# A hybrid encoder layer: the output projection in seven block products, with weight sums formed by GpSimd during attention

## The chip, the cores and the metric

The kernel runs on one core of one Trainium2 chip. The time is device microseconds of one execution; the time of a kernel is the median of its runs. The engines are TensorE (PE, with its weight loads as PEld), VectorE (DVE), ScalarE (ACT), GpSimd (POOL) and SyncE (SP); the last two and ScalarE can issue DMA transfers, which 16 DMA engines carry out.

## The reference

A layer of a streaming encoder on 512 tokens of width 2048, with 16 learned meta tokens ahead of them. The normed input is multiplied by an input matrix; its columns feed two mixers side by side. The first is a Mamba-2 state-space mixer with 32 heads (convolution over time, decay, chunks of 64 tokens), the second a windowed attention with 16 query heads, 4 key heads and sinks. Their outputs, 2048 and 1024 wide, are set side by side and multiplied by the output matrix:

```
mix = concat([y, att])            # 512 tokens x 3072
out = mix @ w_out                 # 3072 x 2048
h = h + rmsnorm(out, norm_post_w) # norm over the 2048 columns of a token
```

All data are float32 and the products must keep nearly that precision.

## The kernel before

**Precision.** Every large product is made of three matmuls on TensorE: each operand is split into hi (rounded to the type float32r) and lo (the rest), and hi x hi, hi x lo and lo x hi are accumulated in one PSUM bank. Weights come in chunks of 128x1024 (512 KB). `load` (L114) issues a chunk's DMA on SP's queue into one of two `st` buffers, `split_w` (L126) lets ScalarE cast it to `hi` (L132) and VectorE subtract `lo` (L133), each with three buffers. `use(n)` (L137) hands out chunk n, splits up to chunk n+2 and loads up to n+4.

**Stages.** A prologue norms and transposes the input. Then 68 tiles of 128 columns of the input projection follow, two chunks each (`project`, L166, matmuls at L157): 4 for keys and values, 16 for queries and gates of the 8 pairs of attention heads (the attention stage), then 48 for the state-space mixer (the SSD stage: per group a tile for cT, one for bT and two each for x and z). Small matmuls of attention and SSD run between these tiles as tasks: a generator gives up control with the planned time until its next piece, `tick` (L101) moves a planned clock on with every group of projection matmuls, and `wake` runs the tasks that are due. This fixes the order in which instructions are handed to the scheduler of the kernel's language, which allots buffers and places each instruction on its engine's in-order queue, where an instruction that could start early may be placed ahead of others. The `steps` task (L386) works out decays on VectorE and ScalarE at the start of attention. In the SSD stage `conv` (L615) copies a tile from PSUM to one of two buffers `ub`, forms four taps on VectorE into a buffer with the tag cT, bT or xs, and uses the buffer `th` for a tanh (L627), which VectorE multiplies in (L628). These buffers lie in the pool `vpool`, which the attention stage uses only at its start (dtT in an xs buffer). GpSimd issues the loads of rows R (L674) and ev (L717) and does one multiplication per SSD unit, `xe` (L713).

**Output projection.** The mixers' outputs lie in 24 tiles `mix[k]` of 128 features x 512 tokens, attention first. For each of four blocks of 512 columns (r), for each of 12 weight chunks (two rows of 128 features) and four tiles of 128 tokens, three matmuls of 128x512 accumulate into four banks (L880); `splitting` (L779) makes hi and lo of `mix` once. At the end of a block VectorE multiplies by the weights of the norm and ScalarE squares and sums (L894, L895); with the last block the inverse root follows, and a scaling with the residual added and the output's store (`finish`, L839; L850, L851).

Of the kernel before, what the change touches and what calls it, by code (L numbers as in the profile page):

```python
# [7 lines left out]
F32 = mybir.dt.float32  # L8
# [19 lines left out]
NST = 2  # L28

# [14 lines left out]
def hybrid_layer(ctx, tc, x, pre, npre, w_in, w_dt, par, w_out, npost, cst, out):  # L44
# [65 lines left out]
    NCH = NCI + 4 * (NKO // 2)  # L110
    staged, ready = {}, {}
    nload, nsplit = [0], [0]

    def load(upto):  # L114
        while nload[0] < min(upto, NCH):
            n = nload[0]
            st = wpool.tile([P, 1024], F32, tag="st", bufs=NST, name=f"st{n}")
# [19 lines left out]
    def use(n):  # L137
        split_w(n + (2 if n == NCI else 3))
        load(n + 3 + NST)
# [361 lines left out]

    keys(0, pieces0)
# [9 lines left out]
    def attend(hp, pieces):  # L512
# [82 lines left out]
        m = mapool.tile([P, S], F32, tag="m", bufs=8, name=f"ma{hp}")  # L595
        nc.vector.scalar_tensor_tensor(m, av, 0.5, gates[hp], ALU.mult, ALU.mult)
        mix[hp] = m
# [12 lines left out]
    ub = [vpool.tile([P, T + 3], F32, name=f"ub{i}") for i in range(2)]  # L610
# [22 lines left out]
    pools = {}  # L633
# [54 lines left out]
    def unit_task(u_, xs, cT):  # L688
# [84 lines left out]
        nc.vector.reciprocal(sq, sq)  # L773
        for v, yt in ((u_ - 1, y0), (u_, yy)):
            m = pools["y"].tile([P, S], F32, tag="m", bufs=16, name=f"my{v}")
            nc.vector.scalar_tensor_tensor(m, yt, hw[:, v:v + 1], sq, ALU.mult, ALU.mult)
            mix[8 + v] = m

    def splitting(ks):  # L779
        for k in ks:  # L780
            mh[k] = o_pool(k).tile([P, S], F32R, name=f"mh{k}")
            ml[k] = o_pool(k).tile([P, S], F32R, name=f"ml{k}")
            nc.scalar.copy(mh[k], mix[k])  # L783
            nc.vector.tensor_tensor(ml[k], mix[k], mh[k].bitcast(F32), ALU.subtract)
# [31 lines left out]
    mh, ml = [None] * NKO, [None] * NKO  # L816
    vpool.release()
    xpool.release()
    o1 = ctx.enter_context(sb("o1", reuse_waits="tile"))
    o2 = []  # L820
    xr = [None] * NT

    def o_pool(k):
        if k < 16:
            return o1
        if not o2:
            assert not tasks
            pools["s"].release()
            o2.append(tc.alloc_tile_pool(name="o2", bufs=1, side="right", reuse_waits="tile"))
        return o2[0]  # L830

    with tc.high_priority(offset=400):
        splitting([0, 1])
    npw = ssq = None
    ot = {}
    n3 = None
    NC = NKO // 2

    def finish(t, jk):  # L839

        b = 3
        rs = o1.tile([P, 2], F32, tag="ors", bufs=4, name=f"ors{t}")
        nc.vector.tensor_reduce(rs[:, 0:1], ssq[:, t, 0:3], AX.X, ALU.add)
        nc.vector.tensor_scalar(rs[:, 0:1], rs[:, 0:1], 1.0 / D, EPS, ALU.mult, ALU.add)
        nc.scalar.activation(jk, pss[t], AF.Square, accum_out=ssq[:, t, 3:4])
        nc.scalar.activation(rs[:, 1:2], ssq[:, t, 3:4], AF.Sqrt, bias=rs[:, 0:1], scale=1.0 / D)
        nc.vector.tensor_tensor(ot[b, t], pss[t], npw[:, b * 512:(b + 1) * 512], ALU.mult)
        nc.vector.reciprocal(rs[:, 1:2], rs[:, 1:2])
        for b in range(4):
            nc.vector.scalar_tensor_tensor(ot[b, t], ot[b, t], rs[:, 1:2], xr[t][b], ALU.mult, ALU.add)  # L850
            nc.sync.dma_start(out[t * P:(t + 1) * P, b * 512:(b + 1) * 512], ot[b, t])  # L851

    for r in range(4):
        b = r
        toks = range(NT)
        pool = wk if b % 2 else pj
# [120 lines left out]
```

## Time and profile before

| | |
|---|---|
| median of 3 runs | 1204.9 us (1203.27 to 1205.04) |
| the profiled execution | 1202.08 us |
| its span, first to last instruction | 1200.3 us |
| mean granted clock of TensorE | 0.998 |
| busy: PE, DVE, ACT, POOL | 99%, 56%, 37%, 4% |
| moved by DMA | 125.53 MB, of them 12.59 MB on GpSimd's queue |

The profile is of one execution. Its own time is a little over its span, as work before the first and after the last instruction is counted. A busy share is a mean over stages. The granted clock is given as a share of the full clock, 2.4 GHz.

### The profile page before, as it was taken

The numbers are of one execution on the slowest core, as the hardware profiler recorded it, in microseconds if no ns is written. First come the engines' busy times: TensorE is split into PE (matmuls) and PEld (weight loads), VectorE is DVE, ScalarE is ACT, GpSimd is POOL, SyncE is SP. The second block draws the span as 40 slices with busy tenths as digits, with TensorE's granted clock in tenths as the row PEclk, the third lists the DMA queues.
The fourth block names the chain that finished last, engine by engine and source line by source line (L and its number), as shares of the span: only waits on it lengthen the run. The fifth ranks groups of instructions, "written<-read, shape, count | busy, mean of one in ns | idle before, by whom it ended". The sixth has DMA issues, their size and how long they took to land.

```text
span 1200.3 us, 18242 instructions
## 1 busy us (share of the span) xinstructions
PE 1188.5 (99%) x7565; PEld 1057.5 (88%) x7565; DVE 676.5 (56%) x1196; ACT 442.9 (37%) x754; POOL 48.6 (4%) x84
## 2 busy tenths in 40 slices
PE   9999999999999999999999999999999999999997
PEld 7998888888999989999999899998997888888886
DVE  7655555555556766757658566676666923232325
ACT  7544544445322423324234233242332612121212
POOL 0000000000000001010000000100100000000000
PEclk9999999999999999999999999999999999999999
DMA  6222222222333233233332332323332432323534
GB/s 240 94 93 88 72 87 71 71 88 85 111 104 115 83 103 107 87 115 97 106 100 95 106 106 88 118 92 105 100 98 79 150 94 99 97 97 99 165 102 178
DMA packets 37044, 125.53 MB, mean 105 GB/s; under 512 B 4705, under 2 KB 5345, under 8 KB 36705
## 3 DMA queue, kind: packets, MB, share of 16 engines
q1 hardware_dynamic: 32864, 111.78, 28.4%
q0 software_dynamic: 4096, 12.59, 3.5%
q8 instruction: 59, 0.97, 0.3%
q14 instruction: 23, 0.19, 0.0%
q10 hardware_dynamic: 2, 0.01, 0.0%
HBM read 120.03 MB, written 4.33 MB: 104 GB/s over the span
## 4 chain that ended last, share of the span: by engine, by line
PE 95%; DVE 2%; ACT 1%; DMA 1%; issue 0%; DVEq 0%; SPq 0%; ACTq 0%
PE pa L157 46%; PE po L880 22%; PE pb L157 16%; PE yd L722 1%; PE av L590 1%; PE stp L732 1%; PE yo L745 1%; PE ptp L572 1%; PE xt L228 1%; PE sc L542 1%; PE cbp L649 1%; PE xp L702 1%; PE sc L541 1%; PE stp L730 1%; PE nw L295 0%
## 5 line engine op out<-in xcount | busy, mean ns | idle before, releaser
L133 DVE TENSOR_TENSOR lo<-st,hi 128x1024 fp32r<-128x1024 f32 x182 | 222.7, 1224 | 378.3 <-ACT hi L132 371.5
L157 PE MATMUL pa<-xh,hi 128*128 128x272 f32 (+2 forms) x1088 | 373.4, 343 | 0.0
L132 ACT CAST hi<-st 128x1024 fp32r<-128x1024 f32 x182 | 191.4, 1052 | 471.0 <-PE po L880 169.3
L157 PE MATMUL pa<-xl,hi 128*128 128x272 f32 (+2 forms) x1088 | 365.0, 335 | 0.0
L157 PE MATMUL pa<-xh,lo 128*128 128x272 f32 (+2 forms) x1088 | 364.6, 335 | 0.0
L157 PEld LDWEIGHTS pa<-xh,hi 128*128 128x128 f32 x1088 | 205.7, 189 | 23.5 <-issue 3.9
L157 PEld LDWEIGHTS pa<-xh,lo 128*128 128x128 f32 x1088 | 205.5, 189 | 20.4
L157 PEld LDWEIGHTS pa<-xl,hi 128*128 128x128 f32 x1088 | 205.7, 189 | 18.1
L157 PE MATMUL pb<-xh,lo 128*128 128x256 f32 x576 | 162.8, 283 | 0.0
L157 PE MATMUL pb<-xh,hi 128*128 128x256 f32 x576 | 162.7, 283 | 0.0
L157 PE MATMUL pb<-xl,hi 128*128 128x256 f32 x576 | 162.7, 282 | 0.0
L880 PE MATMUL po<-hi,mh 128*128 128x512 f32 x384 | 149.5, 389 | 1.2 <-ACT mh L783 1.2
L880 PE MATMUL po<-lo,mh 128*128 128x512 f32 x384 | 149.4, 389 | 0.0
L880 PE MATMUL po<-hi,ml 128*128 128x512 f32 x384 | 148.9, 389 | 0.0
L157 PEld LDWEIGHTS pb<-xh,hi 128*128 128x128 f32 x576 | 108.5, 188 | 1.0
L157 PEld LDWEIGHTS pb<-xl,hi 128*128 128x128 f32 x576 | 108.4, 188 | 0.0
L157 PEld LDWEIGHTS pb<-xh,lo 128*128 128x128 f32 x576 | 108.4, 188 | 0.0
L880 PEld LDWEIGHTS po<-hi,mh 128*128 128x128 f32 x384 | 72.1, 188 | 16.3 <-ACT mh L783 1.4
L880 PEld LDWEIGHTS po<-hi,ml 128*128 128x128 f32 x384 | 72.1, 188 | 15.1
L880 PEld LDWEIGHTS po<-lo,mh 128*128 128x128 f32 x384 | 72.1, 188 | 14.9
L626 DVE SCALAR_TENSOR_TENSOR cv<-ub,pr,cv 128x528 f32<-128x528 f32 (+1 forms) x96 | 73.4, 764 | 2.4
L627 ACT ACTIVATE ct<-cv 128x528 f32<-128x528 f32 (+1 forms) x32 | 20.5, 641 | 67.0 <-DVE cv L626 66.9
(210 smaller groups left out, 1067.8 us busy)
## 6 DMA issues: line engine op xcount, KB each, us to landing
st<-in_w_in SPq DMA_DIRECT2D x136, 512.0 KB, 3.7
st<-in_w_out SPq DMA_DIRECT2D x48, 512.0 KB, 3.6
R<-scr POOLq DMA_DIRECT2D x32, 256.0 KB, 3.7
x<-in_x SPq DMA_DIRECT2D x8, 512.0 KB, 8.5
ev<-scr POOLq DMA_DIRECT2D x32, 128.0 KB, 3.0
out<-o SPq DMA_DIRECT2D x16, 256.0 KB, 2.4
xr<-in_x SPq DMA_DIRECT2D x8, 256.0 KB, 6.0
npw<-in_npost SPq DMA_DIRECT2D x1, 1024.0 KB, 4.2
```

Source lines behind the costliest of these rows:

```text
L132: nc.scalar.copy(hi, st)
L133: nc.vector.tensor_tensor(lo, st, hi.bitcast(F32), ALU.subtract)
L157: nc.tensor.matmul(ps, wt, xt[k][:, a:b], start=(k == 0 and j == 0), stop=(k == NKT - 1 and j == 2))
L228: nc.tensor.transpose(tp[:, kk, :], xts[j][:, k * P:(k + 1) * P], ident)
L541: nc.tensor.matmul(sv[:, c, o0:o1], lq, kh[:, kv, t0:t0 + o1 - o0], start=True, stop=False)
L542: nc.tensor.matmul(sv[:, c, o0:o1], lq, kl[:, kv, t0:t0 + o1 - o0], start=False, stop=True)
L572: nc.tensor.transpose(tp[:, sl * P:(sl + 1) * P], src, ident)
L590: nc.tensor.matmul(av[h * 64:h * 64 + 64, j * P:(j + 1) * P], lt, rh, start=(s_ == 0), stop=(s_ == 1))
L626: nc.vector.scalar_tensor_tensor(d, uu[:, tap + c0:tap + T], cw[:, ct, tap:tap + 1], d, ALU.mult, ALU.add)
L627: nc.scalar.activation(th[:, 0:n], d, AF.Tanh)
L649: nc.tensor.matmul(cbp[:, j * P:(j + 1) * P], bT[:, cs], cT[:, cs], start=True, stop=True)
L880: nc.tensor.matmul(pss[t], a[k][:, cs], w_, start=(k == 0 and i == 0), stop=(k == NKO - 1 and i == 2))
```

## The change

The product of the 512 x 3072 `mix` and the 3072 x 2048 weights is cut into two halves along each of its three dimensions: tokens (LO and HI, 256 each), features (12 tiles each) and columns (1024 each). Instead of the eight products of blocks, seven products of sums of blocks are formed (a Strassen-Winograd scheme), each of 256 tokens x 1536 features x 1024 columns, accumulated in four banks.

- **Weight sums.** Four of the seven products need sums of weight blocks. The task `weight_sums` is started at the beginning of attention, before `keys(0)`. In 24 steps it loads pieces of the four blocks (128x512, 256 KB each) on GpSimd's queue, adds them there in four operations, and stores each sum to DRAM (`wsum`) from the same queue. It borrows the buffers cT, xs, th or bT, and `ub`, in two alternating sets; the loads of a step are handed out one step ahead. The two `ub` buffers are now made at that point.
- **Weights.** The output projection loads 7 x 12 chunks from `w_out` or `wsum`. Two more `st` buffers come from the pool `o1` once it is open.
- **Activations.** `mix` tiles are now pairs (128 x 2 x 512). `held` forms the sums of activations for each product on VectorE (s1, s2 and in-place differences) and splits the result into `ah` and `al`, up to two pairs of features ahead.
- **Blocks.** `done` combines each finished bank into the blocks of the output: copies on ScalarE after the first product, additions and subtractions on VectorE after the others, then `weigh` (square on ScalarE, weights of the norm on VectorE). Blocks of the first 256 tokens are complete after the sixth product, those of the others after the seventh, and `finish` scales, adds the residual and stores them.

The core of the diff:

```diff
+KH = NKO // 2
-    NCH = NCI + 4 * (NKO // 2)
+    NCH = NCI + 7 * KH
+    wsum = dpool.tile([4, 2, KH // 2, P, 1024], F32, name="wsum")
+    def w_block(rows, cols):
+        return w_out[2 * cols:2 * cols + 2, rows * KH // 2:(rows + 1) * KH // 2]
+    W_SRC = [w_block(0, 0), wsum[1], w_block(1, 0), wsum[0], wsum[2], w_block(1, 1), wsum[3]]
     def load(upto):
...
+            if n % 4 > 1 and "o" in pools:
+                st = pools["o"].tile([P, 1024], F32, tag="st", bufs=2, name=f"st{n}")
+            else:
+                st = wpool.tile([P, 1024], F32, tag="st", bufs=NST, name=f"st{n}")
...
-                src = w_out[(n - NCI) // (NKO // 2), (n - NCI) % (NKO // 2)]
+                m = (n - NCI) % KH
+                src = W_SRC[(n - NCI) // KH][m % 2, m // 2]
...
-        load(n + 3 + NST)
+        load(n + 3 + (4 if "o" in pools else NST))
...
+    ub = [vpool.tile([P, T + 3], F32, name=f"ub{i}") for i in range(2)]
+    def weight_sums():
+        w11, w12, w21, w22 = [w_block(r, q) for r in range(2) for q in range(2)]
+        sets = {}
+        def at(n):
+            return n // 2 % 2, n // 4, slice(None), slice(512 * (n % 2), 512 * (n % 2) + 512)
+        def fetch(n):
+            tags = (("cT", 2), ("xs", 2), ("th", 1) if n % 2 else ("bT", 1))
+            v = [vpool.tile([P, T], F32, tag=tag, bufs=bufs, name=f"ws{n}_{m}") for m, (tag, bufs) in enumerate(tags)]
+            sets[n] = [t[:, 0:512] for t in v + [ub[n % 2]]]
+            for to, fr in zip(sets[n], (w22, w12, w11, w21)):
+                if n < 2:
+                    tc.keep_in_program_order(nc.vector.memset(to[:, 0:1], 0.0))
+                nc.gpsimd.dma_start(to, fr[at(n)])
+        fetch(0)
+        yield 5.0
+        for n in range(2 * KH):
+            if n + 1 < 2 * KH:
+                fetch(n + 1)
+            td, tb_, ta, tc_ = sets.pop(n)
+            for m, to, other in ((2, td, tb_), (0, tb_, ta), (1, ta, td), (3, tc_, ta)):
+                nc.gpsimd.tensor_tensor(to, to, other, ALU.add)
+                nc.gpsimd.dma_start(wsum[m][at(n)], to)
+            yield 9.8
+    spawn(weight_sums(), 6.0)
     keys(0, pieces0)
...
+    def sums(i):
+        h1, h2 = mix[i], mix[NP + i]
...
+        nc.vector.tensor_tensor(s1[i], h2[:, :, HI], h1[:, :, HI], ALU.subtract)
+        nc.vector.tensor_tensor(s2[i], s1[i], h1[:, :, LO], ALU.add)
+    def held(p, i):
+        h1, h2 = mix[i], mix[NP + i]
+        if p == 1:
+            sums(i)
+        elif p == 4:
+            nc.vector.tensor_tensor(h1[:, :, HI], h1[:, :, LO], h1[:, :, HI], ALU.subtract)
+        elif p == 5:
+            nc.vector.tensor_tensor(s2[i], s2[i], h2[:, :, LO], ALU.subtract)
+        src = (h1[:, :, LO], s2[i], h2[:, :, LO], s1[i], h1[:, :, HI], s2[i], h2[:, :, HI])[p]
...
+        nc.scalar.copy(ah, src)
+        nc.vector.tensor_tensor(al, src, ah.bitcast(F32), ALU.subtract)
+        return ah, al
+    def weigh(t, b, src):
...
+        nc.scalar.activation(jk, src, AF.Square, accum_out=ssq[:, t, n:n + 1])
+        nc.vector.tensor_tensor(oo[t, b], src, npw[:, b * 512:(b + 1) * 512], ALU.mult)
+    def finish(t, last):
+        nc.scalar.activation(rs[t][:, 1:2], ssq[:, t, 3:4], AF.Sqrt, bias=rs[t][:, 0:1], scale=1.0 / D)
+        nc.vector.reciprocal(rs[t][:, 1:2], rs[t][:, 1:2])
+        for b in [b for b in range(4) if b != last] + [last]:
+            nc.vector.scalar_tensor_tensor(oo[t, b], oo[t, b], rs[t][:, 1:2], xr[t, b], ALU.mult, ALU.add)
+            nc.sync.dma_start(out[t * P:(t + 1) * P, b * 512:(b + 1) * 512], oo[t, b])
+    def done(p, t, b, ps):
+        if p == 0:
...
+            nc.scalar.copy(oo[t, b], ps)
+        elif p == 1:
...
+            nc.vector.tensor_tensor(uu[t, b], ps, oo[t, b], ALU.subtract)
+        elif p == 2:
+            c = oo[t, b]
+            nc.vector.tensor_tensor(c, ps, c, ALU.add)
+            weigh(t, b, c)
+        elif p == 3:
...
+            nc.vector.tensor_tensor(vv[t, b], uu[t, b], ps, ALU.subtract)
+        elif p == 4:
...
+            nc.vector.tensor_tensor(c, vv[t, b], ps, ALU.subtract)
+            nc.vector.tensor_tensor(uu[t, b], ps, uu[t, b], ALU.subtract)
+            weigh(t + 2, b + 2, c)
+        elif p == 5:
...
+            nc.vector.tensor_tensor(c, c, ps, ALU.subtract)
+            weigh(t, b + 2, c)
+            if b == 1:
+                finish(t, 3)
+        else:
...
+            nc.vector.tensor_tensor(c, ps, c, ALU.add)
+            weigh(t + 2, b, c)
+            if b == 1:
+                finish(t + 2, 1)
+    tb = [(t, b) for t in range(2) for b in range(2)]
+    for p in range(7):
+        pss = {v: bank((pj, wk)[p % 2], f"po{p}_{v[0]}{v[1]}") for v in tb}
+        last = 3 if p == 6 else 1
+        order = [(i, t) for i in range(KH - last) for t in range(2)]
+        order += [(i, t) for t in range(2) for i in range(KH - last, KH)]
+        wts = {}
+        for i, t in order:
+            if i not in wts:
+                wts[i] = use(NCI + p * KH + i)
+                if i % 2 == 0:
+                    n = p * NP + i // 2
+                    for m in range(n + 1, min(n + 3, 7 * NP)):
+                        if m not in ops:
+                            ops[m] = held(m // NP, m % NP)
...
+            for kk in range(2):
+                ws = slice(kk * 512, (kk + 1) * 512)
+                for j, (a, w_) in enumerate(((ah, hi), (ah, lo), (al, hi))):
+                    nc.tensor.matmul(pss[t, b], a[:, kk, cs], w_[:, ws], start=(i < 2 and kk == 0 and j == 0),
+                                     stop=(i >= KH - 2 and kk == 1 and j == 2))
...
+            if i >= KH - 2:
+                done(p, t, b, pss[t, b])
```

Here b is `i % 2`: chunk i holds two rows of 128 features (kk) of one block of 512 columns.

## Rows read from the trace of the kernel before

**Rows 1.** The page, part 1: TensorE's busy us, share, instructions.
```profile
PE 1188.5 (99%) x7565; PEld 1057.5 (88%) x7565; DVE 676.5 (56%) x1196; ACT 442.9 (37%) x754; POOL 48.6 (4%) x84
```

**Rows 2.** Busy time by stage: us and instructions by engine, clock, DMA.
```profile
0.00:20.00 20.00, 17.19 (x71) 11.48 (x72) 12.82 (x37) 12.97 (x27) 0.20 (x4) 1.00 0.85 312
55.00:310.00 255.00, 254.91 (x1548) 218.25 (x1547) 139.85 (x308) 125.94 (x286) 4.38 (x8) 1.00 0.27 87
...
930.00:1180.00 250.00, 249.19 (x1099) 206.36 (x1100) 86.88 (x99) 71.04 (x98) 0.00 (x0) 1.00 0.35 112
```

**Rows 3.** Chain that ended last, in time: start us, us, what.
```profile
943.12 249.57 PE po L880 x1101
```

**Rows 4.** Timeline of the end, TensorE and VectorE: start us, us.
```profile
1192.29 0.39 PE L880 MATMUL po<-hi,ml 128*128 128x512 f32 x1
...
1194.23 2.74 DVE L850 SCALAR_TENSOR_TENSOR o<-o,ors,xr 128x512 f32<-128x512 f32 x4
```

**Rows 5.** Groups by line: busy us, mean ns | idle before, releaser.
```profile
L133 DVE TENSOR_TENSOR lo<-st,hi 128x1024 fp32r<-128x1024 f32 x182 | 222.7, 1224 | 378.3 <-ACT hi L132 371.5 <-DMA xr<-in_x 3.6 <-PE ptp L572 2.7
...
L132 ACT CAST hi<-st 128x1024 fp32r<-128x1024 f32 x182 | 191.4, 1052 | 471.0 <-PE po L880 169.3 <-PE pb L157 168.9 <-PE pa L157 65.0
...
L850 DVE SCALAR_TENSOR_TENSOR o<-o,ors,xr 128x512 f32<-128x512 f32 x16 | 11.0, 748 | 0.1
...
L784 DVE TENSOR_TENSOR ml<-my,mh 128x512 fp32r<-128x512 f32 x16 | 10.0, 680 | 0.0
...
L895 DVE TENSOR_TENSOR o<-po,npw 128x512 f32<-128x512 f32 x12 | 8.3, 690 | 5.0 <-ACT ojk L894 5.0
```

**Rows 6.** DMA issues: queue, count, KB, median us to landing.
```profile
R<-scr POOLq DMA_DIRECT2D x32, 256.0 KB, 3.7
...
out<-o SPq DMA_DIRECT2D x16, 256.0 KB, 2.4
```

**Rows 7.** The line that loads weights: min/median/max, issue and landing.
```profile
L122 SPq DMA_DIRECT2D st<-in_w_out x48: 327/327/328, 901.9 to 1167.9; - x48
...
DMA to landing us min/median/max: 3.3/3.6/9.0
```

**Rows 8.** Views of single tiles and lines: ns min/median/max.
```profile
L674 POOL DMA_DIRECT2D R<-scr x32: 538/545/710, 289.5 to 854.1; - x32
...
L713 POOL TENSOR_TENSOR xe<-xd,dte x16: 828/830/1222, 351.9 to 914.4; 128x384 f32<-128x384 f32 x16
...
L626 DVE SCALAR_TENSOR_TENSOR cv<-ub,pr,cv x96: 741/754/1226, 315.8 to 904.5; 128x528 f32<-128x528 f32 x72, 128x512 f32<-128x512 f32 x24
```

**Rows 9.** Groups of VectorE in attention, 200 to 255.26 us.
```profile
L133 DVE TENSOR_TENSOR lo<-st,hi 128x1024 fp32r<-128x1024 f32 x8 | 9.8, 1223 | 16.0 <-ACT hi L132 16.0
...
L557 DVE TENSOR_SCALAR pbuf<-pbuf,sm 128x192 f32<-128x192 f32 (+2 forms) x16 | 3.7, 303 | 0.1
L522 DVE TENSOR_TENSOR qs<-qr,qs 64x512 fp32r<-64x512 f32 x4 | 2.7, 686 | 0.1
...
L471 DVE TENSOR_TENSOR qr<-qr,swq 128x512 f32<-128x512 f32 x2 | 1.4, 694 | 0.1
```

**Rows 10.** Timeline of GpSimd, its first loads and xe.
```profile
299.53 2.07 POOL L717 DMA_DIRECT2D ev<-scr  x4
351.88 0.83 POOL L713 TENSOR_TENSOR xe<-xd,dte 128x384 f32<-128x384 f32 x1 [50.28 <-DVE xd L710]
```

**Rows 11.** Timeline of VectorE in the steps task.
```profile
61.58 0.32 DVE L415 SCALAR_TENSOR_TENSOR da<-dt,ea 128x160 f32<-128x160 f32 x1
```

**Rows 12.** Timeline of VectorE at the first convolution.
```profile
318.84 0.69 DVE L628 SCALAR_TENSOR_TENSOR cv<-ct,cv 128x512 f32<-128x512 f32 x1 [0.50 <-ACT ct L627]
...
321.81 1.22 DVE L133 TENSOR_TENSOR lo<-st,hi 128x1024 fp32r<-128x1024 f32 x1
```

**Rows 13.** Timeline of ScalarE's weight casts, same stretch.
```profile
320.70 1.04 ACT L132 CAST hi<-st 128x1024 fp32r<-128x1024 f32 x1
...
332.25 1.04 ACT L132 CAST hi<-st 128x1024 fp32r<-128x1024 f32 x1
```

More of the change, by code (lines that the diff above doesn't have):

```diff
@@ L607, in hybrid_layer @@
         gates[hp] = gs
-    ub = [vpool.tile([P, T + 3], F32, name=f"ub{i}") for i in range(2)]
     for t in ub:
@@ L632, in hybrid_layer @@
     cdv = cdec.rearrange("p (j h) -> p j h", h=NH)
-    pools = {}
     def open_pools():
@@ L773, in unit_task @@
         nc.vector.reciprocal(sq, sq)
+        mix[4 + g] = pools["y"].tile([P, 2, S], F32, tag="m", bufs=8, name=f"my{g}")
         for v, yt in ((u_ - 1, y0), (u_, yy)):
[L775 to L784, printed above, removed]
+            nc.vector.scalar_tensor_tensor(mix[4 + g][:, v % 2], yt, hw[:, v:v + 1], sq, ALU.mult, ALU.mult)
     for g in range(8):
@@ L834, in hybrid_layer @@
[L834 to L851, printed above, removed]
@@ new lines, in hybrid_layer, with o_tile @@
+    ops = {}
+    with tc.high_priority(offset=400):
+        ops[0] = held(0, 0)
+    npw = o1.tile([P, D], F32, name="npw")
+    nc.sync.dma_start(npw, npost.partition_broadcast(P))
+    ssq = o1.tile([P, NT, 4], F32, name="ssq")
+    uu, vv, oo, xr, rs = {}, {}, {}, {}, {}
+    def o_tile(name):
+        return pools["c"].tile([P, S], F32, name=name)
+    def weigh(t, b, src):
+        n = b if t < 2 else (0, 3, 1, 2)[b]
+        jk = o1.tile([P, S], F32, tag="jk", bufs=1, name=f"jk{t}_{b}")
+        nc.scalar.activation(jk, src, AF.Square, accum_out=ssq[:, t, n:n + 1])
+        nc.vector.tensor_tensor(oo[t, b], src, npw[:, b * 512:(b + 1) * 512], ALU.mult)
@@ new lines, in residual @@
+    def residual(t):
+        pool, nb = (mapool, 4) if t < 2 else (pools["y"], 8)
+        for h in range(2):
+            xq = pool.tile([P, 2, S], F32, tag="m", bufs=nb, name=f"xr{t}_{h}")
+            nc.sync.dma_start(xq.rearrange("p a b -> p (a b)"), x[t * P:(t + 1) * P, h * 1024:(h + 1) * 1024])
+            xr[t, 2 * h], xr[t, 2 * h + 1] = xq[:, 0], xq[:, 1]
+    def finish(t, last):
[4 more added lines that the diff above has]
+            nc.sync.dma_start(out[t * P:(t + 1) * P, b * 512:(b + 1) * 512], oo[t, b])
@@ new lines, in hybrid_layer @@
+    tb = [(t, b) for t in range(2) for b in range(2)]
[13 more added lines that the diff above has]
+                            ops[m] = held(m // NP, m % NP)
+                if p == 5 and i in (0, 2):
+                    residual(i // 2)
+                if p == 6 and i in (2, 4):
+                    residual(1 + i // 2)
+            hi, lo = wts[i]
+            ah, al = ops[p * NP + i // 2]
+            b = i % 2
+            cs = slice(t * P, (t + 1) * P)
+            for kk in range(2):
[3 more added lines that the diff above has]
+                                     stop=(i >= KH - 2 and kk == 1 and j == 2))
+                tick(0.68)
+            if i >= KH - 2:
+                done(p, t, b, pss[t, b])
@@ L907, in hybrid_layer @@
+    pools["c"].release()
     pools["y"].release()
```

99 lines of the change are left out of this document (30 added, 69 removed).

## The prediction

> **What bounds the kernel now.** I read the page first, then busy time by stage, then the chain that ended last, and after that the groups of each engine. TensorE is busy 99% of the span, and the granted clock is 1.00 in each stage read, the 2.4 GHz level [rows 1, 2]. The chain is TensorE almost throughout, and its last long piece is the output projection: 1101 matmuls in 249.57 us without a break, 0.2267 us each; behind the last matmul, which ends at 1192.68, come 7.6 us of VectorE and output stores up to the span's end at 1200.3 [rows 3, 4]. So in this stage time is the number of matmuls, as long as what feeds TensorE keeps up. VectorE is busy there 86.88 of 250 us, GpSimd not at all; in the attention stage GpSimd is busy 4.38 of 255 us and the DMA engines 27% [rows 2]. The change takes work from the one full engine and gives it to idle ones.
>
> **The sum: matmuls.** Before, the projection has 4 x 24 x 4 x 3 = 1152 matmuls, after it 7 products x 12 weight chunks x 2 token tiles x 2 rows of 128 x 3 terms = 1008, all of the same 128x128 by 128x512 shape. 144 x 0.2267 = 32.6 us less, 228.5 us for the stage.
>
> **VectorE in the projection.** Each chunk now feeds 12 matmuls (2.72 us) instead of 24 (5.44 us), and there are 84. VectorE pays 84 lo at 1.22 = 103 us; 42 splits of activations at 0.68 = 29; 24 sums of activations at 0.68 (two for each of six pairs in the second product, one in the fifth and the sixth) = 16; 44 operations on output blocks at 0.69 = 30; 16 last scalings at 0.75 = 12 [rows 5]. That is 190 of 228.5 us, 83% instead of 35%. On the mean it fits; what costs is bunching at the end of a product. Three hi/lo buffers mean that a chunk is split while the chunk two before it runs: two chunks, 5.4 us, less hi 1.05 and lo 1.22, so a lo may come 3.1 us late. From the end of a product's first bank (three banks of 6 matmuls, 4.1 us, before its end) to the need for the third chunk of the next lie 4.1 + 5.4 = 9.5 us. After the sixth product VectorE has there 8 x 0.69 + 8 x 0.75 + 2 x 1.22 + 0.68 = 14.6 us, 5 too many; after the fifth 12 x 0.69 + 2 x 1.22 + 2 x 0.68 = 12.1, 2.6 too many; after the third 8.6. Lost: between 0 (a lo goes ahead of the block work) and 8; I take 3, since recorded durations overlap a little when operations stand back to back (the last four scalings take 2.74 us together, four means 2.99 [rows 4, 5]). ScalarE pays 84 hi at 1.05 and some 0.6 us pieces and is no limit. SP issues 36 loads more at 0.33 us, each [rows 7], about 28 us in all on a queue that issues nothing else but outputs and x there; 512 KB every 2.72 us are 193 GB/s, and at the start of the kernel the DMA engines moved 312 at a share of 0.85 [rows 2].
>
> **The end.** The last bank now needs one addition (0.69) ahead of the square; the multiplication by the weights then runs beside the square instead of behind it (0.3 back): +0.4 us.
>
> **The sums in attention: cost of a step.** There are 24 steps of 4 loads, 4 additions of 128x512 and 4 stores, all on GpSimd's in-order queue, which before holds only the R and ev loads and xe. An addition: xe, 128x384 with two SBUF inputs, is 0.83 us [rows 8], in proportion 1.11 (from 0.83, if all were fixed, to 1.11). An issue of 256 KB from this queue is 0.545 [rows 8]; the rows have only loads on it, and I take a store as the same. 4 x 1.11 + 8 x 0.545 = 8.8 us, a step's floor. Semaphore hops between an addition and its store and back: 8 at 0 to 0.2, no row shows one, I take 0.1: +0.8. Then VectorE. Once xe took 1.222 instead of 0.83 and a cv beside it 1.226 instead of 0.754 [rows 8]: two operations with two SBUF inputs delayed each other. In two rounds of attention, 55.26 us, lo, the pbuf scalings, the second half of qs and the last sum of the rotation, all with SBUF inputs alone, hold VectorE 9.8 + 3.7 + 2.7 + 1.4 = 17.6 us, 32% [rows 9]; an addition that meets one waits up to 1.22 us, about half an operation on the mean: 0.32 x 0.6 = 0.2, +0.8 a step (0 to 4.9). Step: 10.4 us.
>
> The Trainium skill ("SBUF — State Buffer", on the two physically separate sides) says that a VectorE instruction with two SBUF inputs and a GpSimd instruction that reads SBUF exclude each other for the whole instruction. The one late xe agrees in kind: both were stretched by 0.4 to 0.5 us. By that rule at its worst, an addition blocked every time, the step would be 14.5 us instead of 10.4, and the change would lose, as the third rival shows.
>
> **The wait for the buffers.** Two sets of four buffers alternate, so the loads of step n+1 wait for the stores of step n-1 to land. A store of 256 KB from SP lands in 2.4 us, a 256 KB load on GpSimd's queue in 3.7 [rows 6]. If all four loads stand at the head of the step, the fourth waits 0.545 + 3.7 - 3 x 0.545 = 2.6 us at most with all additions behind it. But GpSimd's order isn't that of the code: the ev loads of units 0 and 1 were issued at 299.53, ahead of xe of unit 0 at 351.88 [rows 10]. The planner puts an instruction where it thinks its inputs ready, so an addition should fill the gap: I take 0 and keep 2.6. The stage moves 50.3 MB more in about 260 us, 193 GB/s, beside 87: at 322 GB/s a full share (87 / 0.27) that is 87%. The start of the kernel ran at 85%, and loads there landed in up to 9.0 us instead of 3.6 [rows 2, 7]; the next loads have almost a step, 10 us, so this is hidden.
>
> **Where the chain of sums ends, and what waits for it.** The first loads wait for VectorE's memsets, kept behind the steps task, whose last operation of the first part ran at 61.58 [rows 11]. 61.9 + 3.7 + 24 x 10.4 + 3.7 for the last landing = 319. The borrowed buffers (cT, xs, th, bT, ub) are those of the convolutions. The first one's tanh writes th, and VectorE's operation that waits for it, at 318.84, stands in order ahead of the lo at 321.81 [rows 12]. A chunk's cast runs when the chunk two before it starts, so this chunk, cast at 320.70, is wanted about when the cast two later runs, at 332.25 [rows 13]; its lo ends at 323.03. So 9.2 us of lateness are free: the chain may end at 318.84 + 9.2 = 328, and each microsecond beyond is TensorE's. The first convolution's copies to ub and the R loads behind the sums on GpSimd's queue lie inside the same bound. At 10.4 us a step nothing is lost; the limit is 10.4 + 9 / 24 = 10.8, a narrow margin. What VectorE loses to GpSimd in attention (32% of its time can be blocked by additions that hold 43%) lengthens softmax by 1 to 2 us in a round of 27.6; the hi and lo casts have room. I take 1 us for the stage (0 to 3).
>
> **Sum.** -32.6 + 3 + 0.4 + 1 = -28.2 us on the profiled execution's 1202.1. The median of the runs is 1204.9, 2.8 above it: 1177. No row says that the new kernel would keep that distance; it is within the spread of the runs.
>
> **Rivals.** First, the sums end late by less than the gain: with hops or lock at twice what I took, 11.3 us a step, the end is 61.9 + 3.7 + 271 + 3.7 = 340, 12 past 328: 1189. For it: most terms of a step are estimates and each tenth counts 24 times. Second, VectorE bounds the projection: bunching at each product's end at the upper bound of 8, and as much at its start, where 9 us of the last SSD unit's work are left to it: +10 to 13 on my 3: 1188. Against it: 17% of free time over the stage. Third, on the other side: the wait of the fourth load comes each step, 10.4 + 2.6 = 13.0 us, the chain ends at 381, 53 us late: 1230. It decides where the step exceeds 10.8 + 28 / 24 = 12.0 us. For it: in-order queue, stores and loads slower at 87% DMA share; against it: the planner's freedom shown in [rows 10]. The full lock (14.5 us a step, end 417, 89 us late: 1266) is its far end and hardly likely, since the median xe was not delayed [rows 8]. Fourth, that the change does not do what it says (TensorE's matmuls slower when fed twice as fast, at 0.234 us: 1008 x 0.0073 = 7 us): 1184; nothing in the rows speaks for it.
>
> **Chances and range.** Forecast 0.50; first rival 0.16; second 0.09; third 0.21; fourth 0.04. The forecast's own range is 1171 (nothing bunches, no delay) to 1187 (all bounds short of the late chain). For 8 in 10 I go from 1171 to 1218, which leaves out the far part of the third rival and a little below. Faster by over 0.2% (2.4 us, about what runs of this kernel can tell from no change): the forecast, the first, second and fourth rivals, less the part of the first that comes near 12 us: 0.75. Within: 0.04, slower 0.21.
>
> **What the changed profile would show.** 1008 matmuls of the projection at 0.227; VectorE above 80% there, with TensorE's gaps only behind the fifth and sixth products, waiting for lo. On GpSimd 96 additions of 1.1 to 1.4 us and 192 issues of 0.55, the last between 300 and 328, and no wait of VectorE, ScalarE or TensorE for it behind 310. The prediction is wrong if steps stand 12 us or more apart, if the loads of a step wait for DMA, if TensorE stands still between 320 and 400, or if lo comes late in every product.

## The result and the profile after

The changed kernel takes 1280.8 us (median of 4 runs, 1277.3 to 1283.0), the kernel before 1204.7 in the same comparison: a ratio of 1.064 [1.0625, 1.0654]. It is 6.4% slower, where 2.3% faster was forecast. The profiled span grew from 1200.3 to 1281.2, by 80.9 us; the profile is of the longest of the four runs.

The page's first part for the changed kernel answers to [rows 1].

```profile
PE 1167.9 (91%) x7421; PEld 1038.1 (81%) x7421; DVE 824.1 (64%) x1310; ACT 492.4 (38%) x812; POOL 273.7 (21%) x372
```

TensorE has 144 matmuls fewer and is now idle for 9% of a longer span. Busy time by stage says where; the columns are those of [rows 2] (stretch, its length, then TensorE, weight loads, VectorE, ScalarE and GpSimd with their counts, granted clock, DMA share, GB/s).

```profile
55.00:310.00 255.00, 206.99 (x1180) 174.61 (x1178) 160.50 (x222) 93.02 (x202) 187.09 (x241) 0.93 0.69 225
310.00:400.00 90.00, 42.68 (x247) 35.53 (x248) 33.09 (x69) 26.17 (x63) 38.73 (x49) 0.71 0.43 137
1045.00:1265.00 220.00, 218.72 (x963) 180.29 (x962) 167.70 (x197) 115.04 (x149) 0.00 (x0) 1.00 0.65 213
```

The projection is as full as before; attention, with GpSimd busy 187 of 255 us, is not. The chain that ended last [rows 3] gives the projection's start, and the timeline of TensorE its last matmul.

```profile
1038.43 11.22 PE po L994 x48
...
1050.10 155.05 PE po L994 x684
```

```profile
1269.39 0.39 PE L994 MATMUL po<-hi,al 128*128 128x512 f32 x1
```

The projection runs from 1038.43 to 1269.78, 231.4 us; before it ran from 930.80, its first matmul in the timeline, to 1192.68, 261.9. Behind the last matmul stand 11.4 us instead of 7.6. So the 80.9 us are 107.6 lost ahead of the projection, 30.5 won in it and 3.8 lost behind it. The next view, TensorE's waits (engine, operation, whom it waited for, us in all, times, the longest), shows the loss.

```profile
PE ptm L610 <- DVE pbuf L604: 71.6, 1, 71.6
PE ptp L619 <- DVE pm L612: 8.8, 4, 3.9
PE tr L455 <- ACT ec L451: 5.4, 1, 5.4
PE ptp L619 <- DVE pbuf L604: 5.4, 2, 3.8
PE sc L588 <- DVE qs L569: 4.1, 2, 2.4
```

There is one stop of 71.6 us, from 285.7 to 357.3, and 23.7 us of short ones. All of them end at VectorE's part of the softmax, the rotation or the steps task (the 5.4 us at ScalarE's ec, which itself waits for VectorE's ec at 76.17, 3.80 us long). Another 1.2 us are longer waits in the prologue. The remaining 11 of the 107.6 us are put down to the granted clock, though no run sets it apart from the stops: it was 1.00 in attention before [rows 2], the 2.4 GHz level, and is 0.93 and 0.71 on the mean in the two stretches that hold the stops.

The timeline of VectorE over the long stop follows; in brackets stands the idle time ahead, and what ended it.

```profile
273.52 1.23 DVE L147 TENSOR_TENSOR lo<-st,hi 128x1024 fp32r<-128x1024 f32 x1 [0.32 <-ACT hi L146]
345.27 0.23 DVE L593 TENSOR_REDUCE mx<-sc 128x1 f32<-128x80 f32 x1 [70.52 <-issue]
345.29 0.06 DVE L659 MEMSET ub<- 128x3 f32 x1
...
352.33 0.36 DVE L593 TENSOR_REDUCE mx<-sc 128x1 f32<-128x192 f32 x1 [2.29 <-DMA wsum<-ub]
352.33 0.06 DVE L659 MEMSET ub<- 128x3 f32 x1
```

VectorE stands still for 70.5 us ahead of a softmax. The profile names no releaser ("issue"), but the next operation in VectorE's queue tells it. This is that queue in program order, from the instruction list of the changed kernel (line, operation, tiles):

```
L147 TENSOR_TENSOR lo_2618<-st_2481,hi_2617 128x1024
L659 MEMSET ub_554 128x3
L593 TENSOR_REDUCE mx_2653<-sc_0_2657 128x1 x2
...
L659 MEMSET ub_553 128x3
```

L659 clears the three columns to the left of each `ub` buffer for the convolutions. In the kernel before, these two memsets run at 1.0 us, at the kernel's start. Now `ub` is also one of the four buffers of a step of sums, `ub_553` of the even steps and `ub_554` of the odd ones, so each memset must wait for what the sums did to its buffer before; the planner placed both in the sixth of eight rounds, and VectorE executes in order. GpSimd's timeline of the last steps:

```profile
341.49 0.54 POOL L534 DMA_DIRECT2D ub<-in_w_out  x1 [2.28 <-DMA wsum<-ub]
...
349.93 0.56 POOL L545 DMA_DIRECT2D wsum<-ub  x1
...
353.19 1.27 POOL L544 TENSOR_TENSOR ub<-ub,ws 128x512 f32<-128x512 f32 x1
354.76 0.56 POOL L545 DMA_DIRECT2D wsum<-ub  x1 [0.30 <-POOL ub L544]
```

The first memset, of `ub_554`, runs at 345.29, 3.8 us after the last step's load into that buffer was issued (such loads land in 3.9 us on the median). The second, of `ub_553`, runs at 352.33, 2.4 us after the last store from that buffer; there the profile names the store (`wsum<-ub`). The first one also does harm to the values: it stands between the last load and its addition at 353.19, so the last sum lacks one of its summands in three columns, and the addition then overwrites the cleared columns of `ub_554`. The edit of e1 below takes away this too.

The groups of VectorE from 100 to 200 us (count, then busy us, mean ns) answer to [rows 9]:

```profile
L147 DVE TENSOR_TENSOR lo<-st,hi 128x1024 fp32r<-128x1024 f32 x12 | 21.3, 1790 | 10.9 <-ACT hi L146 10.8
L604 DVE TENSOR_SCALAR pbuf<-pbuf,sm 128x192 f32<-128x192 f32 (+2 forms) x24 | 19.3, 877 | 0.1
L569 DVE TENSOR_TENSOR qs<-qr,qs 64x512 fp32r<-64x512 f32 x6 | 7.3, 1213 | 1.5 <-ACT qs L568 1.4
L594 DVE TENSOR_SCALAR ng<-mx,pr 128x2 f32<-128x2 f32 x12 | 7.2, 600 | 0.3
...
L484 DVE TENSOR_TENSOR swq<-swq,rt 128x512 f32<-128x512 f32 x3 | 3.7, 1244 | 0.0
L483 DVE TENSOR_TENSOR qr<-pa,rt 128x512 f32<-128x512 f32 x3 | 2.1, 688 | 1.1 <-ACT swq L481 1.0
```

lo went from 1.223 to 1.790 us, pbuf from 0.303 to 0.877, qs from 0.686 to 1.213 [rows 9]; swq, 0.68 before, takes 1.244. The operations with an input in PSUM (qr from `pa`, and gs with 0.674) keep 0.67 to 0.69. Three rounds of attention run in these 100 us (24 pbuf scalings), where before there were four (16 in two rounds, [rows 9]).

The groups of GpSimd over the whole span, with the idle time ahead and its releasers, answer to [rows 6, 8]:

```profile
L544 POOL TENSOR_TENSOR ws<-ws,ws 128x512 f32<-128x512 f32 x72 | 93.1, 1303 | 14.7 <-DMA ws<-in_w_out 13.6
L545 POOL DMA_DIRECT2D wsum<-ws x72 | 39.8, 553 | 3.0 <-issue 2.7 <-POOL ws L544 0.3
...
L534 POOL DMA_DIRECT2D ub<-in_w_out x24 | 13.1, 544 | 42.1 <-DMA wsum<-ub 41.7 <-issue 0.4
```

An addition takes 1.30 us, an issue 0.55, and the fourth load waits 41.7 / 24 = 1.7 us a step for the store of its buffer. The timeline of GpSimd puts the fourth store of the first step at 81.60 and that of the last at 354.76 (shown above):

```profile
81.60 0.54 POOL L545 DMA_DIRECT2D wsum<-ub  x1
```

(354.76 - 81.60) / 23 = 11.9 us a step, where 10.4 was forecast.

### The profile page after: what moved, and what is told of

Read it like the earlier page. It is cut to its first block, busy times and chain, and to the rows that moved or that the text cites. A ratio compares the mean times of both kernels' runs of the same rounds, so it can differ in the third digit from the quotient of the medians.

```text
span 1281.2 us, 18679 instructions
## 1 busy us (share of the span) xinstructions
PE 1167.9 (91%) x7421; PEld 1038.1 (81%) x7421; DVE 824.1 (64%) x1310; ACT 492.4 (38%) x812; POOL 273.7 (21%) x372
## 5 line engine op out<-in xcount | busy, mean ns | idle before, releaser
L147 DVE TENSOR_TENSOR lo<-st,hi 128x1024 fp32r<-128x1024 f32 x218 | 281.5, 1295 | 240.8 <-ACT hi L146 232.0
L146 ACT CAST hi<-st 128x1024 fp32r<-128x1024 f32 x218 | 228.9, 1050 | 365.3 <-PE pb L171 169.6
L994 PE MATMUL po<-lo,ah 128*128 128x512 f32 x336 | 131.1, 390 | 1.3 <-DVE lo L147 1.3
L994 PE MATMUL po<-hi,ah 128*128 128x512 f32 x336 | 129.7, 389 | 1.2 <-ACT ah L886 1.2
L994 PE MATMUL po<-hi,al 128*128 128x512 f32 x336 | 130.2, 389 | 0.0
L544 POOL TENSOR_TENSOR ws<-ws,ws 128x512 f32<-128x512 f32 x72 | 93.1, 1303 | 14.7 <-DMA ws<-in_w_out 13.6
L759 POOL TENSOR_TENSOR xe<-xd,dte 128x384 f32<-128x384 f32 x16 | 13.6, 853 | 331.4 <-DVE xd L756 331.4
L994 PEld LDWEIGHTS po<-lo,ah 128*128 128x128 f32 x336 | 63.1, 188 | 15.3 <-DVE lo L147 2.4
L994 PEld LDWEIGHTS po<-hi,ah 128*128 128x128 f32 x336 | 63.1, 188 | 14.5 <-ACT ah L886 1.4
```

What stands on the lines that cost most here:

```text
L146: nc.scalar.copy(hi, st)
L147: nc.vector.tensor_tensor(lo, st, hi.bitcast(F32), ALU.subtract)
L544: nc.gpsimd.tensor_tensor(to, to, other, ALU.add)
L759: nc.gpsimd.tensor_tensor(xe, xd[:, 0:NT - 1], dte[:, 0:NT - 1, h0:h0 + 2].unsqueeze(3).to_broadcast([P, NT - 1, 2, 64]), ALU.mult)
L994: nc.tensor.matmul(pss[t, b], a[:, kk, cs], w_[:, ws], start=(i < 2 and kk == 0 and j == 0), stop=(i >= KH - 2 and kk == 1 and j == 2))
```

## The experiments

The theory after the result: two separate things cost the time, the place of the memset in VectorE's queue, and GpSimd's additions, which hold up VectorE. Rivals: the sums are just late (the third rival), the transfers are what slows attention, or the products are worth less than thought. The time of the kernel before was 1204.0 to 1204.4 us in all comparisons below.

**e1: the memset freed.** The sums use columns 3 to 514 of `ub`, so that the memset of columns 0 to 2 depends on nothing and is again at the head of the queue.

```diff
-            sets[n] = [t[:, 0:512] for t in v + [ub[n % 2]]]
+            sets[n] = [t[:, 0:512] for t in v] + [ub[n % 2][:, 3:515]]
```

> One edit: the sums use columns 3 to 514 of each ub buffer instead of 0 to 511, so that the memset of its first three columns has nothing to wait for. Theory (order): TensorE's stop of 72 us is VectorE standing in order at this memset, which the planner put three rounds ahead of the end of attention; without it attention runs on, the sums end near 358 us as before, and the first convolution, at about 335 us there, has its 28 us of slack: 1204 us (1197 to 1210). Rival (lateness): the sums end 30 us past the 328 us that the prediction allowed, whichever instruction waits for them; the stop moves to the first convolution's th: 1230 to 1240 us.

Measured: 1232.9 us (1223.2 to 1237.7), 1.023 [1.0176, 1.0286], slower than before but with runs 14 us apart; span 1235.9, of one of the two longest runs. TensorE's longest waits:

```profile
PE ptp L619 <- DVE pm L612: 15.7, 4, 4.7
PE sc L588 <- DVE qs L569: 12.2, 3, 5.2
PE ptm L610 <- DVE pbuf L604: 5.4, 3, 4.6
```

The long stop is gone, though the sums end as late as before (last store issued at 354.32); nothing on TensorE waits for a sum. So the stop was the memset's place. Neither the expected 1204 us nor the rival's stop at the first convolution came. Only 48 us came back: the short waits grew, as attention now runs beside the additions nearly to its end. The first product begins at 993.13, 62 us later than in the kernel before.

**e2: transfers without additions.** e1 with all 96 loads and 96 stores, and no addition; the stored sums are unsummed pieces.

```diff
-                nc.gpsimd.tensor_tensor(to, to, other, ALU.add)
```

> As e1_ub_shift, without the 96 additions of GpSimd (the loads and stores stay, so that wsum holds unsummed blocks). Theory (shared port): TensorE's short stops in attention, about 20 us besides the long one, come from VectorE operations held up by GpSimd's additions; they go: 1184 us, and the sums' loop ends by 270 us. Rival (DMA): they come from 190 GB/s more of transfers, w_in chunks landing late; they stay: 1204 us.

Measured: 1177.0 us in one run, 7 below what was expected, span 1175.2. Busy time from 100 to 200 us, and the same stretch's first group of VectorE:

```profile
100.00:200.00 100.00, 100.00 (x569) 83.49 (x568) 57.36 (x134) 49.20 (x119) 44.29 (x82) 1.00 0.91 286
```

```profile
L147 DVE TENSOR_TENSOR lo<-st,hi 128x1024 fp32r<-128x1024 f32 x15 | 18.4, 1224 | 21.9 <-ACT hi L146 19.1 <-PE ptp L618 2.7
```

TensorE is full at a DMA share of 0.91, and lo has its old duration. The transfers alone cost next to nothing: 1.8 us more than e3, which has none.

**e3: the products alone.** No sums at all; the chunks of the four products that need sums are read from blocks of `w_out`, so their weights are not the sums.

```diff
-    spawn(weight_sums(), 6.0)
-    W_SRC = [w_block(0, 0), wsum[1], w_block(1, 0), wsum[0], wsum[2], w_block(1, 1), wsum[3]]
+    W_SRC = [w_block(0, 0), w_block(0, 1), w_block(1, 0), w_block(1, 1), w_block(0, 1), w_block(1, 1), w_block(1, 0)]
```

> The seven products alone: no weight sums at all, the chunks are read from blocks of w_out. The projection and the end as after, attention as before: 1204.9 - 34.6 (projection, 261.9 to 227.3 us) + 7.9 (end) = 1178 us (1174 to 1182). If the projection's gain hangs on something in attention (or the start of the SSD stage is late for another reason), it is above 1185.

Measured: 1175.2 us (1174.8 to 1176.6), 0.9765 [0.9749, 0.9782]; span 1172.8. The first product begins at 930.84 (before: 930.80), the last matmul ends at 1162.19. The gain that the change was after is there, as expected, and all of the loss comes from the sums: 1280.8 - 1175.2 = 105.6 us, of which e1's edit returns 48 and 58 remain.

**e4: the additions without transfers.** e3 with the 96 additions on GpSimd, on eight buffers loaded once; nothing is stored.

```diff
+                if n < 2:
+                    nc.gpsimd.dma_start(to, fr[at(n)])
-                nc.gpsimd.dma_start(wsum[m][at(n)], to)
```

> As e3_products_only with GpSimd's 96 additions in attention, on buffers loaded once, without the loads and stores of the steps. Shared port: the short stops of attention stay, 1178 + 20 = 1198 us. DMA as their cause: 1178 us.

Measured: 1206.5 us in one run (1198 was expected), span 1204.7, 31.9 over e3's. The additions stand back to back, 1.47 us each on the mean, and are done at 209 us. Busy time, and groups of VectorE from 100 to 200 us:

```profile
100.00:200.00 100.00, 84.87 (x430) 67.50 (x428) 88.76 (x100) 38.95 (x92) 100.00 (x71) 0.93 0.16 53
```

```profile
L606 DVE TENSOR_SCALAR pbuf<-pbuf,sm 128x192 f32<-128x192 f32 (+2 forms) x24 | 28.2, 1242 | 0.1
L146 DVE TENSOR_TENSOR lo<-st,hi 128x1024 fp32r<-128x1024 f32 x12 | 24.2, 2028 | 7.8 <-ACT hi L145 7.7
```

At a DMA share of 0.16 VectorE is stretched more than in the changed kernel. The additions alone do it; transfers aren't needed. The operations with an input in PSUM keep their durations here too (qr from `pa` 0.687). That e4 loses less than e1 ahead of the projection, 32 us against 62, fits the number of rounds that meet additions: from one round's first transpose (`ptm`) to the next it takes 32.5, 38.0 and 37.1 us (24.9, 28.3 and 27.6 before) and then 27.6 again, while in e1 five of the seven distances are longer, by 5 to 15 us.

**e5: sums by the DMA engines.** Copies from DRAM to DRAM and accumulating transfers, no addition on an engine.

```diff
-                nc.gpsimd.tensor_tensor(to, to, other, ALU.add)
-                nc.gpsimd.dma_start(wsum[m][at(n)], to)
+            nc.gpsimd.dma_start(wsum[2][at(n)], w12[at(n)], accum_op=ALU.add, max_dma_last_dim=2048)
+            nc.gpsimd.dma_start(wsum[0][at(n)], w11[at(n)], accum_op=ALU.add, max_dma_last_dim=2048)
...
```

> The sums without any engine: in 12 steps DRAM-to-DRAM copies of blocks of w_out into wsum, and accumulating DMAs that add the other block, all on GpSimd's queue, paced by one-element writes that wait for a small memset; no buffers borrowed, no addition on GpSimd. The result is complete. Shared port: no engine reads SBUF for the sums, so VectorE keeps its durations and attention runs as before: 1175 to 1183 us. Rival (traffic, or GpSimd's queue held up by landings ahead of R and ev loads): TensorE stops in attention or early in the SSD stage, 1195 us or more.

Measured: 1244.3 us (1243.6 to 1246.7), 1.034 [1.0319, 1.0353]; the expected 1175 to 1183 was far off, and the rival came. Busy time from 100 to 300 us and TensorE's longest wait:

```profile
100.00:200.00 100.00, 96.23 (x542) 80.35 (x541) 47.90 (x110) 44.03 (x101) 23.46 (x36) 0.98 0.90 223
200.00:300.00 100.00, 79.42 (x426) 64.76 (x425) 40.40 (x100) 37.18 (x91) 26.48 (x42) 0.90 0.83 210
```

```profile
PE pa L171 <- ACT hi L146: 21.9, 1, 21.9
```

This moves the cost elsewhere. GpSimd waits for its own landings (85.5 us for `wsum<-wsum`, 70.2 for `wsum<-in_w_out`), and that reaches TensorE through VectorE's in-order queue too, as its timeline shows:

```profile
229.62 0.06 DVE L527 MEMSET ub<- 1x1 f32 x1 [15.03 <-DMA wsum<-ub]
...
396.46 0.29 DVE L727 TENSOR_SCALAR R<-R,acs 128x128 f32<-128x128 f32 x1 [32.98 <-DMA R<-scr]
```

The small memset that paces a step waits for the one-element writes of an earlier step, and VectorE with it, 52.2 us in six waits: the trap of the changed kernel once more, made by the experiment itself. The first loads of R stand on GpSimd's queue behind the last transfers (issued at 388.96), and VectorE waits 33.0 us for them; TensorE's 21.9 us for a cast end there, since this cast stands behind ScalarE's operation on R. And weights land later, from 100 to 400 us in 7.3 us on the median and 17.1 at most, against 5.5 and 8.6 in e2; ScalarE's casts wait 55.1 us for them, in 15 waits. At a share like e2's the engines moved 210 to 223 GB/s instead of 286 to 302. VectorE's operations keep their old durations (lo 1.22, pbuf 0.305), yet TensorE waits 31 us for pm, pbuf and qs: only a duration tells that an operation was stretched, not a wait for it. What sums by the DMA engines cost without the pacing stays open.

**e6: the additions on VectorE.** e1 with the additions on VectorE, and there kept in the order of the code; the transfers stay on GpSimd's queue.

```diff
-                nc.gpsimd.tensor_tensor(to, to, other, ALU.add)
+                tc.keep_in_program_order(nc.vector.tensor_tensor(to, to, other, ALU.add))
```

> As e1_ub_shift, with the 96 additions on VectorE, kept in the order of the code there (so paced by the planned clock); loads and stores stay on GpSimd's queue. Shared port: 96 x 0.69 = 66 us more work for VectorE in 255, but no GpSimd instruction reads SBUF; lo, ng, pbuf keep 1.22, 0.23 and 0.31: 1180 to 1192 us. Rival (any 60 to 70 us more on VectorE's in-order queue in attention costs as much, since e1 lengthened VectorE's work by about as much): 1215 us or more.

Measured: 1185.1 us (1184.4 to 1185.6), 0.984 [0.9826, 0.9856], as expected; span 1182.9. Busy time by stage, and groups of VectorE from 100 to 200 us:

```profile
55.00:100.00 45.00, 38.43 (x270) 36.50 (x269) 29.08 (x56) 19.23 (x34) 17.24 (x32) 0.92 0.76 242
...
100.00:200.00 100.00, 100.00 (x565) 83.47 (x564) 76.42 (x159) 50.06 (x122) 38.64 (x72) 1.00 0.83 272
```

```profile
L544 DVE TENSOR_TENSOR ws<-ws,ws 128x512 f32<-128x512 f32 x27 | 18.6, 688 | 0.5
L147 DVE TENSOR_TENSOR lo<-st,hi 128x1024 fp32r<-128x1024 f32 x14 | 17.1, 1223 | 11.0 <-ACT hi L146 11.0
...
L604 DVE TENSOR_SCALAR pbuf<-pbuf,sm 128x192 f32<-128x192 f32 (+2 forms) x24 | 5.5, 305 | 0.1
```

The busier engine does the work at half the price: 0.688 us an addition instead of 1.30, nothing is stretched, and TensorE is full from 100 us on at 76% of VectorE. What is left is the stretch from 55 to 100 us, with a longest wait of TensorE of 5.0 us, for ScalarE's ec: the steps task's operations stand behind the first additions.

**e7: shorter additions.** e1 with each addition on GpSimd in four pieces of 128x128.

```diff
-                nc.gpsimd.tensor_tensor(to, to, other, ALU.add)
+                for c in range(0, 512, 128):
+                    nc.gpsimd.tensor_tensor(to[:, c:c + 128], to[:, c:c + 128], other[:, c:c + 128], ALU.add)
```

> As e1_ub_shift, each addition in four pieces of 128x128. If a VectorE operation waits for the GpSimd instruction that is running, its mean wait falls with the piece's length (about 0.35 instead of 1.27 us): lo back toward 1.4 us, ng below 0.5, and the time falls to 1205 to 1220 us although GpSimd's busy time is no shorter. If the share of GpSimd's busy time counts, the durations and the 1233 us stay or grow.

Measured: 1238.6 us in one run (1205 to 1220 was expected), span 1236.8. Busy time, a group of VectorE from 100 to 200 us, and TensorE's longest wait:

```profile
100.00:200.00 100.00, 100.00 (x565) 83.50 (x564) 67.77 (x122) 50.92 (x122) 86.27 (x172) 1.00 0.69 227
...
300.00:400.00 100.00, 49.39 (x363) 47.15 (x362) 29.16 (x58) 16.90 (x39) 80.91 (x170) 0.73 0.56 182
```

```profile
L147 DVE TENSOR_TENSOR lo<-st,hi 128x1024 fp32r<-128x1024 f32 x14 | 21.6, 1549 | 20.4 <-ACT hi L146 17.6 <-PE ptp L620 2.7
```

```profile
PE pa L171 <- ACT ub L668: 43.8, 1, 43.8
```

This run separates the two costs. With pieces of 0.51 to 0.53 us VectorE waits so little that TensorE is full from 100 to 300, though GpSimd is busier than in e1. But four pieces take 2.1 us instead of 1.3, the last store is issued at 385.69 instead of 354.32, and now the first convolution really waits for them: 43.8 us at its copy into `ub`.

**e8 and e9: e6 put in order.** e8 starts the sums behind the steps task and spaces them more tightly; e9 is e8 with the last product's end reordered.

```diff
-    spawn(weight_sums(), 6.0)
+    spawn(weight_sums(), 27.0)
-            yield 9.8
+            yield 8.9
```

> The sums of e6 (additions on VectorE), started 21 us of the program's clock later, behind the steps task, and spaced 8.9 instead of 9.8 us so that they end about where they did. In e6 the first product began at 940.67 instead of the 930.84 of the kernel without sums, 9.8 us late, and the profile showed one place for it: the stretch 55 to 100 us, where TensorE waited 6.5 us for the steps task's VectorE operations that stood in order behind the first additions, at a lower clock. If that is the whole of it, the first product begins at 931 to 934 and the time is 1175 to 1179. Rival: additions on VectorE cost wherever they stand (96 x 0.69 = 66 us of its time), or the tighter spacing makes the transfers late: then the gap only moves and the time stays at 1183 to 1190.

```diff
-            if b == 1:
-                finish(t + 2, 1)
+            if b == 1 and t == 1:
+                finish(2, 1)
+                finish(3, 1)
```

> As e8, and in the seventh product the final scalings of the first token tile are written behind the additions of the second token tile, not ahead of them. In the changed kernel the last product's last two additions ran at 1270.73, behind four scalings, though TensorE's last matmul ended at 1269.78, and the span ended 11.4 us behind that matmul (7.6 before the change). If the scalings ahead are what made the end longer, the end is 9 to 10 us and the time 1 to 2 us below e8. Rival: what is left on VectorE behind the last matmul is the same sum of work in another order, and the end stays at 10.5 to 11.5.

Measured: e8 1177.2 us (1176.0 to 1178.3), 0.978 [0.9764, 0.9793]; e9 1175.8 (1175.6 to 1176.8), 0.977 [0.9754, 0.9787], both as expected. In e8 the stretch 55 to 100 us is full, and the first product begins at 933.85:

```profile
55.00:100.00 45.00, 45.00 (x309) 41.74 (x309) 29.92 (x57) 22.74 (x40) 10.87 (x20) 1.00 0.61 196
...
933.85 11.17 PE po L994 x48
```

So nearly 7 of e6's 10 us were that one place; 3 remain against e3's 930.84, and 1.6 in e9 (932.44), which is the same up to there. e9's span ends 9.7 us behind its last matmul, e8's 10.5; the order explains 0.8 us at most, and the difference of the medians is no larger than their spread. e9 has every part of the change and takes as long as e3, which has no sums: with the additions on VectorE and in the right place, the sums are all but free, and the kernel is 2.3% faster than before.

## Why the prediction was wrong

**Right: the products, as a sum.** The forecast for the projection was 228.5 us of matmuls, 3 lost to VectorE's bunching: 231.5. It took 231.4, with two waits for lo (1.3 us) and one for ah (1.2) against TensorE. VectorE was busy 168 of 220 us, 76% where 83% was worked out. e3 and e9 landed at 1175 and 1176, the forecast was 1177. The two waits for lo came behind the fifth and the sixth product, where they were foretold. That the sum fits to 0.1 us is partly luck: the bunching cost 1.3 us instead of 3, and the 1.2 us at the start, which the kernel before has too, were not in the forecast. The fourth rival (slower matmuls) and the second (VectorE as the bound there) didn't happen: 684 matmuls in 155.05 us are 0.2267 each, as before. The ends of the forecast's own range do not come out of its terms: no bunching and no delay give 1173, not 1171, and all bounds 1184, not 1187; nothing hangs on it.

**Mis-sized: the end.** "+0.4" counted one addition. It was +3.8: the last two additions ran at 1270.73, behind four scalings of the other token tile, and the sum of squares and two small operations followed. The multiplication by the weights, taken to run beside the square, still waited for it (1272.21, right behind). e8, with the old order, ended 10.5 us behind its last matmul and e9 9.7, so 2 us remain over the 7.6 of before. Small, and argued from the timeline.

**Mis-sized: the step of sums.** 10.4 us was the forecast, 11.9 the measurement, above the limit of 10.8. The addition was 1.30 instead of 1.11 (+0.8 a step), the issues were right, and the fourth load's wait, taken at 0 with a bound of 2.6, was 1.7. Additions that waited for a load took 0.6 more; the 1.6 for hops and for VectorE's hold did not show as waits of GpSimd. The argument that the planner would fill the gap failed: it moved some loads ahead, but the load of `ub` still stood before the next additions. This is the third rival in kind, at two thirds of its price. But what it held to follow, a late first convolution, didn't: in e1 the sums end where they did, and no wait for them is left, since attention itself has become 62 us longer by then.

**Failed: "Where the chain of sums ends, and what waits for it".** The first waiter was not the convolution's tanh at 318.84 with 9 us of slack. It was a memset that writes three columns of a borrowed buffer. Before, it stood at the start of VectorE's queue and depended on nothing, so no row of the trace showed a wait there. Borrowing `ub` gave it a dependency on the last steps of the sums, and its place in an in-order queue, five rounds into attention, did the rest: 71.6 us (e1 takes it away with the sums just as late). Every writer of a borrowed buffer had to be followed, this one too. The prediction named tanh and the copies into `ub` and overlooked the memset. e7 then shows the bound that had been named: there the copy into `ub` did wait, 43.8 us.

**Failed: what VectorE loses to GpSimd, "1 us for the stage (0 to 3)".** Up to 36 us in the changed kernel go there (107.6 - 71.6: 23.7 of stops, 1.2 in the prologue, the rest put down to the lower clock, some of that right behind the long stop, where it is 0.74 for 10 us); it was 62 in e1 and 32 in e4. Two things were wrong. The wait was charged to the GpSimd addition, half an operation each; but GpSimd's additions stayed at 1.30 (1.26 at the shortest, 1.47 in e4 on the mean), and VectorE waited, for whole additions. Between 100 and 360 us, 30 of the 113 operations lo, pbuf, ng, qs and swq take over 0.15 us longer than the same shape before, 55 us in all. Each of the 30 ends, to 0.2 us, its own former length behind the end of an addition; in e2 and e6, without additions on GpSimd, none is that much longer. Here an ng of 0.23 us takes 4.18 and ends with the third addition:

```profile
211.95 4.18 DVE L594 TENSOR_SCALAR ng<-mx,pr 128x2 f32<-128x2 f32 x1
```

```profile
211.76 2.52 POOL L544 TENSOR_TENSOR ws<-ws,ws 128x512 f32<-128x512 f32 x2
214.21 0.56 POOL L545 DMA_DIRECT2D wsum<-ws  x1
214.79 1.29 POOL L544 TENSOR_TENSOR ub<-ub,ws 128x512 f32<-128x512 f32 x1
```

And the lengthening that was foreseen for VectorE, 1 to 2 us in a round, was taken as covered, since the casts "have room". The row that bore on it was the maximum of [rows 8], not the median: a cv from 0.754 to 1.226. From 100 to 200 us lo, pbuf, qs, ng and swq lost 12 x 0.57 + 24 x 0.57 + 6 x 0.53 + 12 x 0.37 + 3 x 0.56 = 30 us, 10 in each of the three rounds, instead of 1 to 2. The softmax is a chain with TensorE in it, so this is not cover but path: TensorE's waits for pm, pbuf and qs come to 33.6 us in e1 and 17 in e4 (for pm and pbuf), and to nothing from 100 us on in e2 and e6.

The Trainium skill ("SBUF — State Buffer", section "Who interferes with whom") counts among the operations that can contend with GpSimd, besides those with two SBUF inputs, also `tensor_scalar`, which can run in a mode with two ports when its operands meet the conditions. The prediction had pbuf, a `tensor_scalar`, on its list, but not ng, which is one too, nor swq with its two SBUF inputs. This case's traces agree: pbuf went from 0.303 to 0.877, and ng, two elements a row, from 0.23 to 0.60 (1.13 from 200 to 250 us). In the kernel before, pbuf takes 0.262, 0.290 and 0.315 us for 80, 144 and 192 columns, 0.47 ns a column, where qs and lo (0.686 for 512, 1.225 for 1024) take 1.05; this fits a mode with two ports. They also agree on the operations that read PSUM (0.67 to 0.69 throughout). Its "whole instruction" was right too, and the prediction dismissed it as the far end "since the median xe was not delayed". The loss just fell on the other engine: the far end's own number, a step of 14.5 us, never came. Slower had a chance of 0.21, by way of late sums; it came by other ways.

The sum as it stands: the prediction's -28.2, then +71.6 for the memset, +35.0 for the rest ahead of the projection beyond the 1 taken, nearly all of it VectorE in attention, +3.4 for the end and -0.9 for the projection (30.5 won, 29.6 forecast) give the measured +80.9.

## What to carry to other kernels

When a buffer is borrowed, list every instruction that writes it later, however small, and its place in its engine's queue and between the borrower's own steps: one that had no dependency may have been placed anywhere, will now stop all behind it, and may clear what the borrower still needs. An idle engine is not free when its operations hold up those of the engine that paces the critical chain: price an addition there by what it does to the neighbour's operations, from the worst row in which the two met, and compare with just doing it on the neighbour (here 0.69 us on a VectorE that is busy 55% of attention, against 1.30 on an idle GpSimd and 30 to 60 us of delays). When the cost of background work is disputed, run its transfers and its arithmetic apart; two runs settled here what no row of the trace before could.

## What was not expected of the hardware

- GpSimd's additions stretch even the smallest VectorE operation: ng, 128x2, took 0.23 us alone, a mean of 1.13 beside the additions from 200 to 250 us, and 4.18 at most.
- Where stores are issued between the additions, a single VectorE operation can wait for three of them (ng 4.18 us, a pbuf scaling 4.98). In e4, where nothing stands between the additions, each waits for one (no pbuf scaling over 1.37). Why was not found; the issues alone (e2) lengthen no such operation by over 0.15.
- A DMA share of 0.91 at 286 to 302 GB/s for 200 us cost TensorE nothing (e2), while accumulating copies from DRAM to DRAM held the engines at 0.83 to 0.90 for 210 to 223 GB/s, and weights landed in 7.3 us on the median beside them, against 5.5 in e2 (e5).
- A GpSimd addition of 128x512 takes 1.30 us on the mean (most 1.26 to 1.31, 1.08 at the shortest, in e4) and one of 128x128 0.51 to 0.53: pieces of a quarter cost 0.4 of the whole, so shorter pieces are paid for in throughput.
